# A two-layer hybrid decoder trunk: in the first feed-forward block the inverse root moves from GpSimd to Newton's steps on VectorE, the token sums stand earlier on TensorE, and VectorE gets another order of block sums and weight sums

## The chip, the cores and the metric

The kernel runs on one core of a Trainium2 chip. The metric is the device time of one execution in microseconds (us); of several runs the median is given. TensorE (PE) multiplies, VectorE (DVE), ScalarE (ACT) and GpSimd (POOL) work on tiles elementwise, and SyncE (SP) issues most transfers. Each engine takes its instructions in order, and an instruction starts when the semaphores that it waits for have been counted up.

## The reference

512 tokens of width 1024 pass two layers. Each layer is a gated feed-forward block, a mixer (a convolution module in layer 0, sparse attention in layer 1), a second feed-forward block and a gated embedding. What matters here is the very first block:

```python
def rms_norm(x, g):
    xf = x.astype(jnp.float32)
    y = xf * lax.rsqrt(jnp.mean(xf * xf, axis=-1, keepdims=True) + RMS_EPS)
    return (y * g.astype(jnp.float32)).astype(x.dtype)

def swiglu(x, wg, wu, wd):
    return (jax.nn.silu(x @ wg) * (x @ wu)) @ wd

x = x + 0.5 * swiglu(rms_norm(x, ffn1_norm[i]), ffn1_w_gate[i], ffn1_w_up[i], ffn1_w_down[i])
```

The inner width is 2816, that is 22 blocks of 128. All inputs are float32.

## The kernel before, in words

**Layout.** The tokens lie transposed: eight tiles `xs` of 128 features x 512 tokens. The norm's factor of a token is not put on the input. The input times the gain goes through the products, and the factor R (one number per token, spread over all partitions) multiplies the result.

**Precision.** Every float32 operand is split into a rounded part h and a rest l = x - h; a product is three matmuls, h·h, h·l and l·h (`mm3`, lines 356 to 358). ScalarE makes h by a copy with rounding and VectorE makes l by a subtraction. For weights these are lines 292 and 294 (tiles `raw` or `rawx` to `wh` and `wl`).

**The norm's factor.** `square_sum` squares the input tiles on ScalarE (line 430) and adds them up on VectorE (line 432) in the tile `acc`. `rfin` then goes in two stages. The first takes the sums over the features for each token, four matmuls of 128x1 (line 445, `token_sums`), adds 1e-6 (line 467, `v`) and raises to the power -0.5 on GpSimd (line 438, `r`). The second spreads r by four transposes on TensorE (line 451) and copies the result on ScalarE (line 458, `R`).

**Plain blocks and pairs.** The first two of the 22 inner blocks (`PLAIN`) are computed directly: gate and up, eight matmul triples each with 512 columns. When R is there, the gate is multiplied by it (line 600), ScalarE takes its Silu (line 601), VectorE multiplies by the up product (line 558), and the result is split (lines 560 and 561). The other blocks go in pairs by a scheme of seven products of 256 columns instead of eight (`pairs`). It needs block sums of the inputs, made once in a feed-forward block by `right_sums`: copies with the gain (line 480), differences (line 482), split in h and l (lines 490 and 491, tiles `px`). And it needs sums of the weights for each pair: `first_sums` and `combine`, lines 327, 328, 312 and 313 (tiles `sq` and `rawx`), split in lines 330 and 331 (`s1hl`) and 316 and 317. The products are called s (the weights themselves), c, e and d (sums of weights): two of s, two of c, one of e, two of d, for the gate and for the up block. Between them ScalarE copies a bank to the tile `G` (line 503) and VectorE adds (line 502).

**What sets the order.** The code is written in the order in which it wants things; a scheduler then merges this into one fixed queue for each engine by its own estimate of times, and `issue_after(x)` forbids it to place an instruction ahead of x. `high_priority` lifts a step. `ahead` splits weights some units (`HLB`, five buffers of h and l) before their product. The second tile of a pair (`rawx`, two buffers) is loaded again only when the last weight sum of the pair before was read. In the first feed-forward block nothing comes before: the program begins with it, and inputs, weights, squares, block sums and weight sums all arrive in the first 60 us.

## Time and profile before

| | us |
|---|---|
| median of 3 runs | 2021.34 (2021.1 to 2021.44) |
| the profiled execution | 2022.01 |
| its span, first to last instruction | 2020.2 |
| PE busy | 1994.7 (99%) |
| DVE busy | 1558.9 (77%) |
| ACT busy | 1100.5 (54%) |
| POOL busy | 330.7 (16%) |

A row of a timeline gives start and length in us, the engine, the line of the kernel, the operation, the tile written and the tiles read, the count of equal instructions put together, and, in brackets, how long the engine stood idle before and what released it. Consecutive instructions of one engine overlap a little, so the distance between two starts is the cost of the first. A matmul of 512 columns is listed with some 0.39 us though the next starts 0.23 us later. A row of stretches gives the limits, the length, busy time and count of instructions for PE, PEld (weight loads), DVE, ACT and POOL, then the TensorE clock that was granted as a share of full speed, the share of the DMA engines, and GB/s.

### The profile page before, as it was taken

Reading aid. Unit: us, or ns where it says so; the run is one execution under the profiler, and the core shown is the slowest. Engines: PE = TensorE matmul, PEld = TensorE weight load, DVE = VectorE, ACT = ScalarE, POOL = GpSimd, SP = SyncE. Lnnn points to the kernel's source line nnn. Section 1 sums busy time; section 2 is a strip of 40 time slices with the busy share of each in tenths; the row PEclk is TensorE's granted clock in tenths of the full one; section 3 lists DMA queues with packets and bytes.
Section 4 is the critical chain, followed back from the end, with each engine's and each line's share of the span. In section 5 each row is a group of like instructions: output and inputs, shape, how many; then the busy total and the mean of one; then the engine's idle time right before and its main releaser. Section 6 shows DMA issues by size and latency. Waiting matters only on the chain.

```text
span 2020.2 us, 32789 instructions
## 1 busy us (share of the span) xinstructions
PE 1994.7 (99%) x12534; PEld 1789.9 (89%) x12534; DVE 1558.9 (77%) x2751; ACT 1100.5 (54%) x1972; POOL 330.7 (16%) x365
## 2 busy tenths in 40 slices
PE   8999999999999999999999999999999999999998
PEld 7989899888789898988999989887888789898987
DVE  8869777795697796877968868647989796886875
ACT  7535445663565363545644525337888674463543
POOL 0000000352300000012000000557666200000022
PEclk9999999999999999999999999999999999999999
DMA  4332322466325243343232322463323023232241
GB/s 169 105 104 96 126 80 99 181 215 201 131 102 169 90 142 125 97 136 115 84 125 85 121 89 95 152 194 103 94 88 102 27 96 124 95 115 94 94 142 58
DMA packets 79485, 235.16 MB, mean 116 GB/s; under 512 B 8849, under 2 KB 16161, under 8 KB 79329
## 3 DMA queue, kind: packets, MB, share of 16 engines
q1 hardware_dynamic: 78368, 230.69, 34.6%
q8 instruction: 98, 1.61, 0.3%
q0 software_dynamic: 816, 2.33, 0.3%
q14 instruction: 59, 0.48, 0.1%
q10 hardware_dynamic: 144, 0.07, 0.0%
HBM read 214.66 MB, written 16.29 MB: 114 GB/s over the span
## 4 chain that ended last, share of the span: by engine, by line
PE 88%; DVE 8%; ACT 2%; issue 1%; DMA 1%; SPq 0%; DVEq 0%; POOL 0%; ACTq 0%
PE b L356 27%; PE b L357 27%; PE b L358 27%; PE b L821 2%; DVE t L1245 1%; PE b L1180 1%; PE b L1242 1%; PE b L1119 1%; DMA raw<-in_w 1%; DVE s L415 1%; DVE e L1198 1%; DVE t L482 1%; DVE wl L294 1%; DVE px L491 0%; DVE acc L432 0%
## 5 line engine op out<-in xcount | busy, mean ns | idle before, releaser
L356 PE MATMUL b<-s,wh 128*128 128x256 f32 (+1 forms) x1408 | 448.8, 320 | 1.6 <-ACT wh L292 1.0
L357 PE MATMUL b<-s,wh 128*128 128x256 f32 (+1 forms) x1408 | 447.8, 319 | 1.3 <-DVE s L415 0.9
L358 PE MATMUL b<-s,wl 128*128 128x256 f32 (+1 forms) x1408 | 445.9, 318 | 0.1
L292 ACT ACTIVATE wh<-raw 128x1024 fp32r<-128x1024 f32 (+1 forms) x251 | 263.8, 1054 | 256.4 <-PE b L357 171.6
L357 PE MATMUL b<-px,wh 128*128 128x256 f32 (+1 forms) x1112 | 321.0, 289 | 1.0 <-DVE px L491 0.8
L356 PE MATMUL b<-px,wh 128*128 128x256 f32 (+1 forms) x1112 | 321.1, 289 | 0.7 <-ACT G L503 0.7
L358 PE MATMUL b<-px,wl 128*128 128x256 f32 (+1 forms) x1112 | 321.0, 289 | 0.0
L294 DVE TENSOR_TENSOR wl<-raw,wh 128x1024 fp32r<-128x1024 f32 (+1 forms) x205 | 251.2, 1227 | 63.6 <-ACT wh L292 62.7
L356 PEld LDWEIGHTS b<-s,wh 128*128 128x128 f32 x1408 | 268.3, 191 | 21.0 <-ACT wh L292 1.6
L357 PEld LDWEIGHTS b<-s,wh 128*128 128x128 f32 x1408 | 268.1, 190 | 20.1 <-DVE s L415 2.5
L358 PEld LDWEIGHTS b<-s,wl 128*128 128x128 f32 x1408 | 267.4, 191 | 17.9 <-DVE wl L294 0.5
L358 PE MATMUL b<-hid,wl 128*128 128x512 f32 x704 | 275.2, 393 | 0.0
L357 PE MATMUL b<-hid,wh 128*128 128x512 f32 x704 | 275.0, 392 | 0.0
L356 PE MATMUL b<-hid,wh 128*128 128x512 f32 x704 | 269.3, 390 | 0.0
L294 POOL TENSOR_TENSOR wl<-raw,wh 128x1024 fp32r<-128x1024 f32 (+1 forms) x53 | 128.4, 2428 | 709.3 <-ACT wh L292 709.2
L503 ACT ACTIVATE G<-b 128x256 f32<-128x256 f32 x400 | 144.5, 376 | 142.6 <-PE b L358 126.9
L357 PEld LDWEIGHTS b<-px,wh 128*128 128x128 f32 x1112 | 209.1, 188 | 6.4 <-DVE px L491 1.4
L356 PEld LDWEIGHTS b<-px,wh 128*128 128x128 f32 x1112 | 209.2, 188 | 6.1 <-ACT G L503 1.3
L358 PEld LDWEIGHTS b<-px,wl 128*128 128x128 f32 x1112 | 208.8, 188 | 3.8
L357 PEld LDWEIGHTS b<-hid,wh 128*128 128x128 f32 x704 | 132.2, 188 | 29.2
L356 PEld LDWEIGHTS b<-hid,wh 128*128 128x128 f32 x704 | 132.2, 188 | 28.4
L358 PEld LDWEIGHTS b<-hid,wl 128*128 128x128 f32 x704 | 132.2, 188 | 27.3
(246 smaller groups left out, 3642.8 us busy)
## 6 DMA issues: line engine op xcount, KB each, us to landing
raw<-in_w SPq DMA_DIRECT2D x255, 512.0 KB, 3.3
rawx<-in_w SPq DMA_DIRECT2D x80, 512.0 KB, 3.2
tw<-in_tw SPq DMA_DIRECT2D x20, 576.0 KB, 6.7
skew<-table SPq DMA_DIRECT2D x16, 320.0 KB, 5.9
z<-t SPq DMA_DIRECT2D x16, 256.0 KB, 2.2
hid<-z SPq DMA_DIRECT2D x16, 256.0 KB, 4.0
tt<-skew SPq DMA_DIRECT2D x16, 256.0 KB, 3.1
wr<-in_w SPq DMA_DIRECT2D x8, 512.0 KB, 4.1
```

Source lines behind the costliest of these rows:

```text
L292: nc.scalar.activation(h[:, c], t[:, c], AF.Copy)
L294: eng.tensor_tensor(l[:, c], t[:, c], h[:, c].bitcast(F32), op=OP.subtract)
L356: mm(out, sh, mh, start=start, stop=False, **how)
L357: mm(out, sh, ml, start=False, stop=False, **how)
L358: self.lastmm = mm(out, sl, mh, start=False, stop=stop, **how).ins
L415: b = nc.vector.scalar_tensor_tensor(view(l), x, g, view(h.bitcast(F32)), op0=OP.mult, op1=OP.subtract)
L482: sub = lambda o, x, y: nc.vector.tensor_tensor(o, x, y, op=OP.subtract)
L503: copy = lambda o, x: nc.scalar.activation(o, x, AF.Copy)
L821: nc.tensor.matmul(p[:, q * SP:q * SP + SP], T[q][:, d * 128:d * 128 + 128], u[:, q, o:o + SP], start=d == 0, stop=d == LAGS - 1)
L1119: nc.tensor.matmul(P[mh][:, :124], w, B[kk // 4][:, kk % 4, :], start=kk == 0, stop=kk == 15)
L1180: nc.tensor.matmul(p[:, :32 - lo + nk], Q, KT[:, i, "sw".index(b), lo:32 + nk], start=i == 0, stop=i == 1)
L1198: nc.vector.tensor_tensor_reduce(out=dst, in0=src[b], in1=bias, scale=1.0, scalar=3e38, op0=OP.add, op1=OP.min, accum_out=mn[:, a, bi:bi + 1])
```

## The change

Only the first feed-forward block of layer 0 (`first`) is touched, in five places.

1. The root. `root_steps` replaces the power on GpSimd: an integer estimate and three Newton steps, ten VectorE instructions of 128x4 (lines 465 to 469 of the new kernel).
2. The token sums. The first stage of `rfin` is written ahead of the eighth input of the first two blocks, no longer behind the third input of the second gate block (`SUMS_AT` is gone). The second stage, the transposes, stays behind the second gate block.
3. The order of block sums and weight sums. For the first pair the weight sums are no longer made along with the split (`lazy`); they are made when the c weights are due, and their splits and the last sum stand behind the block sums (`issue_after(self.righted)`). `cap` limits how far weights are split ahead in the meantime. The four calls of `right_sums` wait for the accumulator's last addition (the first one) or the end of the root (the others).
4. The plain blocks' gates (R, Silu and so on) are written behind the block sums and the first products of the first pair instead of ahead of them.
5. Six buffers for temporaries (`tb`) in this block instead of four.

```diff
+NEWTON = 3
...
         if pair:
-            with self.behind():
-                self.first_sums(j)
+            if j not in self.lazy:
+                with self.behind():
+                    self.first_sums(j)
+                    self.sum_parts(j)
...
+        lazy = what == "c" and j in self.lazy
+        if lazy:
+            self.first_sums(j)
         q = self.sums[j]
         if what == "c":
             nc.vector.tensor_tensor(q[:, lo], u[:, lo], t[:, lo], op=OP.subtract)
-            nc.vector.tensor_tensor(u[:, lo], t[:, hi], q[:, lo], op=OP.subtract)
+            if not lazy:
+                nc.vector.tensor_tensor(u[:, lo], t[:, hi], q[:, lo], op=OP.subtract)
...
+        if lazy:
+            with self.tc.issue_after(self.righted):
+                self.sum_parts(j)
+                nc.vector.tensor_tensor(u[:, lo], t[:, hi], q[:, lo], op=OP.subtract)
...
+    def root_steps(self, v, n):
+
+        nc = self.nc
+        y = self.tiny.tile([128, 4], F32, name="r", tag="r")[:, :n]
+        a = self.tiny.tile([128, 4], F32, name="ra", tag="ra")[:, :n]
+        nc.vector.tensor_scalar(y.bitcast(I32), v.bitcast(I32), -0.5, float(0x5f3759df), op0=OP.mult, op1=OP.add)
+        for _ in range(NEWTON):
+            nc.vector.tensor_tensor(a, y, y, op=OP.mult)
+            nc.vector.scalar_tensor_tensor(a, a, -0.5, v, op0=OP.mult, op1=OP.mult)
+            self.root = nc.vector.scalar_tensor_tensor(y, a, 1.5, y, op0=OP.add, op1=OP.mult).ins
+        return y
...
-            r = self.rsqrt(v, 4)
+            r = (self.root_steps if steps else self.rsqrt)(v, 4)
...
+        first = (n, i) == (1, 0)
+        if first:
+            self.lazy = [PLACE[nm, i, 0, PLAIN][0] for nm in (g, u)]
+            self.cap = ENTRY["s", self.lazy[0]]
+        fin = self.rfin(self.acc, steps=first)
...
                             plain(pg, g, f, ks)
                             plain(pu, u, f, ks)
+                            if first and len(ks) > 1:
+                                with self.tc.issue_after(self.lastmm):
+                                    next(fin)
...
                 if first:
-                    with self.tc.issue_after(self.squared), self.tc.issue_after(self.vins):
-                        for k in range(KD // 2):
+                    for k in range(KD // 2):
+                        with self.tc.issue_after(self.squared), self.tc.issue_after(self.root if k else self.summed):
                             self.right_sums(f"ffn{n}_norm", i, k)
+                        if k == KD // 2 - 2:
+                            self.cap = ENTRY["s", self.lazy[1]] + 1
+                            with self.tc.issue_after(self.root):
+                                self.ahead(ENTRY["s", self.lazy[1]])
+                    self.cap = None
...
+                if first and f == PLAIN:
+                    with self.tc.issue_after(self.righted):
+                        plain_gates()
...
-            self.tb = 4
+            self.tb = 6 if i == 0 else 4
```

In the built programs the order differs on PE, DVE and ACT within the first feed-forward block alone; GpSimd loses the root, and SyncE's order is the same. Line numbers of the new kernel are larger: 375 to 377 are the old 356 to 358, 476 the old 445, 482 the old 451, 498 the old 467, 513 the old 482, 522 the old 491, 534 the old 503, 639 the old 601.

**PE, around the token sums.** Before, in the second gate block (`b_282`) and the second up block (`b_283`):

```order
L357 MATMUL b_282<-s_180,wh_138 128x512
L358 MATMUL b_282<-s_179,wl_139 128x512
L445 MATMUL b_301<-meanr,acc_183 128x1 x4
L451 MATMUL b_325<-ident,r 128x128 x4
L356 MATMUL b_283<-s_151,wh_144 128x512
```

Now, where the first two blocks (`b_206` and `b_207`) end with their eighth input (`s_179`, `s_180`) and the second gate block (now `b_281`) begins:

```order
L377 MATMUL b_206<-s_179,wl_125 128x512
L376 MATMUL b_207<-s_180,wh_132 128x512
L377 MATMUL b_207<-s_179,wl_133 128x512
L476 MATMUL b_256<-meanr,acc_183 128x1 x4
L375 MATMUL b_281<-s_151,wh_138 128x512
```

The token sums have moved up by the 24 matmuls of the second gate block; the transposes stay behind that block. In the built order the sums stand behind the eighth input of both first blocks.

**DVE, behind the accumulator's last addition.** Before (`acc_183`; then weight sums, splits, `v`, block sums):

```order
L432 TENSOR_TENSOR acc_183<-acc_183,t_203 128x512
L327 TENSOR_TENSOR sq_218<-raw_142,rawx_208 128x512
L328 TENSOR_TENSOR rawx_208<-rawx_208 128x512
L312 TENSOR_TENSOR sq_218<-rawx_208,raw_142 128x512
L294 TENSOR_TENSOR wl_145<-raw_136,wh_144 128x1024
L294 TENSOR_TENSOR wl_215<-raw_142,wh_214 128x1024
L331 TENSOR_TENSOR s1hl_221<-rawx_208,s1hl_221 128x512
L467 TENSOR_SCALAR v<-b_301 128x4
L482 TENSOR_TENSOR t_363<-G_362 128x512
```

Now, the accumulator's last addition is followed by the first block sums, `v` and the root's steps (`r` and `ra`); the third Newton step follows some rows further down:

```order
L451 TENSOR_TENSOR acc_183<-acc_183,t_203 128x512
L513 TENSOR_TENSOR t_339<-G_338 128x512
L513 TENSOR_TENSOR t_340<-G_338,t_339 128x256
L513 TENSOR_TENSOR t_340<-G_338,t_340 128x256
L498 TENSOR_SCALAR v<-b_256 128x4
L465 TENSOR_SCALAR r<-v 128x4
L467 TENSOR_TENSOR ra<-r 128x4
L468 SCALAR_TENSOR_TENSOR ra<-ra,v 128x4
L295 TENSOR_TENSOR wl_145<-raw_136,wh_144 128x1024
L469 SCALAR_TENSOR_TENSOR r<-ra,r 128x4
L467 TENSOR_TENSOR ra<-r 128x4
L522 TENSOR_TENSOR px_346<-t_339,px_346 128x512
```

The weight sums of the first pair have left this place for one behind the root; all eight block sums' splits (`px`) now stand ahead of the first gate times R.

**ACT, around the first Silu.** Before (the plain gate `b_206`, among weight splits `wh` and block sums `px`):

```order
L316 ACTIVATE wh_440<-rawx_208 128x1024
L601 ACT_TABLE_LOAD
L601 ACTIVATE t_418<-b_206 128x512
L316 ACTIVATE wh_473<-rawx_212 128x1024
L292 ACTIVATE wh_504<-raw_290 128x1024
L490 ACTIVATE px_401<-t_392 128x512
L490 ACTIVATE px_412<-t_405 128x512
L503 ACTIVATE G_439<-b_437 128x256
```

Now, between the copies (`G`) of the first pair's banks (`b_402`, `b_405`, and `b_403`, `b_406` for its other sums):

```order
L534 ACTIVATE G_407<-b_405 128x256
L639 ACT_TABLE_LOAD
L639 ACTIVATE t_634<-b_206 128x512
L534 ACTIVATE G_404<-b_402 128x256
L534 ACTIVATE G_407<-b_405 128x256
L639 ACTIVATE t_642<-b_281 128x512
L323 ACTIVATE wh_434<-rawx_208 128x1024
L323 ACTIVATE wh_467<-rawx_212 128x1024
L595 ACTIVATE hid_638<-b_207 128x512
L534 ACTIVATE G_404<-b_403 128x256
```

The table load and the Silu wait for the gate times R on VectorE, and the copies that the pair's next products need are now queued behind them.

## The prediction

> **What bounds the kernel now.** I read the page first, then the timeline of TensorE (PE) over the first 60 us, the stretches with their granted clock, and the timelines of VectorE (DVE) and ScalarE (ACT) beside it. The page gives the span, and 99% of it with PE busy.

> ```profile
> span 2020.2 us, 32789 instructions
> ```

> So what PE loses anywhere reaches the end, and a gain counts only as far as PE stays fed behind it. In PE's timeline (start, length, engine, line, tiles, count, idle time before) the change's place looks so:

> ```profile
> 20.81 0.39 PE L356 MATMUL b<-s,wh 128*128 128x512 f32 x1
> ...
> 26.25 0.95 PE L445 MATMUL b<-meanr,acc 128*128 128x1 f32 x8
> 29.87 1.12 PE L451 MATMUL b<-ident,r 128*128 128x128 f32 x4 [2.67 <-POOL r L438]
> 30.64 0.78 PE L356 MATMUL b<-s,wh 128*128 128x512 f32 x1
> ...
> 38.63 0.28 PE L356 MATMUL b<-s,wh 128*128 128x256 f32 x1
> ...
> 50.03 0.39 PE L356 MATMUL b<-px,wh 128*128 128x256 f32 x2
> 50.56 0.39 PE L357 MATMUL b<-px,wh 128*128 128x256 f32 x1
> 50.78 0.28 PE L358 MATMUL b<-px,wl 128*128 128x256 f32 x1
> 50.90 0.28 PE L357 MATMUL b<-px,wh 128*128 128x256 f32 x1
> 51.02 0.28 PE L358 MATMUL b<-px,wl 128*128 128x256 f32 x1
> 51.54 0.39 PE L356 MATMUL b<-px,wh 128*128 128x256 f32 x1 [0.24 <-ACT G L503]
> ```

> The second gate block (24 matmuls) runs from 20.81 to 26.25, so one of 512 columns costs 0.227 us. Then the token sums, and 2.67 us idle until GpSimd's root; the second up block follows at 30.64, and the products of the first pair of blocks (256 columns, 0.12 us each by 50.78 and 50.90) at 38.63. The idle time costs twice, as the stretches show (length, busy time of PE, PEld, DVE, ACT, POOL, then the granted clock):

> ```profile
> 25.60:29.01 3.41, 1.60 (x12) 1.40 (x10) 3.41 (x6) 0.06 (x1) 0.60 (x1) 1.00 0.40 139
> 29.01:35.84 6.83, 5.97 (x16) 4.88 (x17) 6.83 (x12) 5.84 (x9) 0.80 (x1) 0.50 0.26 85
> 1390.93:1394.35 3.42, 2.00 (x9) 1.28 (x7) 2.38 (x4) 3.42 (x10) 3.42 (x4) 1.00 0.04 14
> 1578.67:1582.08 3.41, 1.00 (x7) 0.55 (x5) 3.35 (x25) 3.36 (x15) 0.91 (x2) 1.00 0.16 65
> 1582.08:1588.90 6.82, 6.34 (x19) 4.56 (x20) 5.05 (x17) 5.90 (x25) 6.08 (x14) 0.50 0.01 4
> ```

> After a stretch with PE busy 1.60 of 3.41 us the clock is halved for 6.83 us, and late in the program once more after 1.00 of 3.41; after 2.00 of 3.42 it is not. PE works 5.97 us of the first halved stretch at half rate, so it loses 3.0 us there. Idle time and half rate together are some 5.6 us: the most that this change can reach for.

> But VectorE is busy in every moment of these two stretches (3.41 of 3.41, 6.83 of 6.83). PE's waits at 50.03 to 51.54 (0.3 us beyond its two matmuls, then 0.4, and 0.1 for each restart, 1.0 in all) already come from there and from ScalarE.

> **Part one: PE's path to the pairs.** The order shown above puts the token sums behind the first blocks' last matmul, not before their eighth input. They read the accumulator, whose last additions and what follows stand in VectorE's timeline:

> ```profile
> 19.81 2.28 DVE L432 TENSOR_TENSOR acc<-acc,t 128x512 f32<-128x512 f32 x3
> 23.23 0.69 DVE L327 TENSOR_TENSOR sq<-raw,rawx 128x512 f32<-128x512 f32 x1 [1.15 <-DMA raw<-in_w]
> ...
> 28.17 0.15 DVE L467 TENSOR_SCALAR v<-b 128x4 f32<-128x4 f32 x1
> 28.24 0.68 DVE L482 TENSOR_TENSOR t<-G 128x512 f32<-128x512 f32 x1
> ...
> 33.99 1.21 DVE L317 TENSOR_TENSOR wl<-sq,wh 128x1024 fp32r<-128x1024 f32 x1
> 35.13 0.68 DVE L482 TENSOR_TENSOR t<-G 128x512 f32<-128x512 f32 x1
> 35.73 1.28 DVE L600 TENSOR_TENSOR b<-b,R 128x512 f32<-128x512 f32 x2
> 36.93 0.41 DVE L482 TENSOR_TENSOR t<-G,t 128x256 f32<-128x256 f32 x1
> 37.26 1.28 DVE L491 TENSOR_TENSOR px<-t,px 128x512 fp32r<-128x512 f32 x2
> ```

> The accumulator is whole at 22.09. That is a new wait: PE, free at 20.81, stands 1.3 us, loads for some 0.15, and everything on its queue stands behind it. Then 0.95 for the sums (23.2), 5.44 for the gate (28.65), the transposes (0.77 at half rate; 0.4 at full), and 5.44 for the up block: the pairs start at 34.5 instead of 38.63, a gain of 4.1 us. The root must be there by 28.65. It is ten VectorE steps of 128x4 behind v. Such a step's cost is bounded by two rows: 0.07 where nothing waits (28.17 to 28.24) and 0.19 where the next needs it:

> ```profile
> 1344.97 0.15 DVE L1215 TENSOR_SCALAR sm<-sm 128x1 f32<-128x1 f32 x1
> 1345.16 0.16 DVE L1216 RECIPROCAL sm<-sm 128x1 f32<-128x1 f32 x1
> ```

> In the order four of the eleven (v counted) have a long instruction behind them, which hides their end, and seven have their reader: 4 times 0.07 and 7 times 0.19, 1.6 us (0.8 to 2.1 at the ends). With the long ones between (one split of 1.14, two px of 0.60) and the three block sums ahead (1.3), the root is there at 22.0 + 1.3 + 1.6 + 2.3 + 0.2 = 27.4. It hides behind the gate with 1.2 us to spare. GpSimd loses a step on which nothing else depends.

> **Part two: VectorE's queue to the first Silu.** What counts is when VectorE ends what PE needs next. Steps by the rows above: 0.60 for 512 columns, 0.33 for 256, 1.14 for 1024. From 22.0 to the first gate times R the new order has 4 block sums of 512 (2.4) and 8 of 256 (2.7), 8 px (4.8), 5 weight splits (5.7), 6 weight sums (3.6), 2 s1hl (1.2): 20.4. With 1.6 for the root, 0.2 for two waits on itself and 0.7 for the gate itself it ends at 44.9. VectorE starts at once on the block sums, where before it stood 1.15 us for a transfer; that pays for most of the root.

> **Part three: ScalarE behind it.** ScalarE's rows are

> ```profile
> 40.32 0.39 ACT L503 ACTIVATE G<-b 128x256 f32<-128x256 f32 x1 [1.80 <-PE b L358]
> 40.60 1.05 ACT L316 ACTIVATE wh<-sq 128x1024 fp32r<-128x1024 f32 x1
> 41.55 1.05 ACT L316 ACTIVATE wh<-rawx 128x1024 fp32r<-128x1024 f32 x1
> 42.62 1.28 ACT L601 ACT_TABLE_LOAD   x1
> 43.91 0.60 ACT L601 ACTIVATE t<-b 128x512 f32<-128x512 f32 x1
> ```

> In the new order the Silu of the plain gate stands ahead of the copies that free the first pair's banks. So: 44.9, table load 1.28, Silu 0.5 to the next start, copy 0.39: PE may go on with the third product (c, second half) at 47.2. PE is there earlier: 34.5, 48 matmuls for s (5.75), 24 for c (2.9, with 0.1 for its last px at 43.0), 24 for e (2.9): 46.1. First wait 1.1. That product runs to 50.1; the next needs a bank that ScalarE copies only after the second copy (0.3), second Silu (0.5), two splits (1.9), a hid (0.5) and the copy (0.4), from 47.0: 50.6. Second wait 0.6. Then VectorE again, from 46.9: up to the second pair's second c split it has 17 steps of 0.60, 6 of 0.33 and 7 of 1.14, 20.2 in all, without a pause: some 67.4. PE has 254 matmuls of 0.12 (30.4) ahead of it: 34.5 + 30.4 + 1.7 + 0.2 for restarts = 66.8. Third wait 0.6 to 0.7.

> **The sum.** 4.1 gained by the pairs' start; 1.0 of old waits gone; 1.1, 0.6 and 0.7 of new ones and 0.3 for restarts: 5.1 - 2.7 = 2.4 us. Behind that the instructions stand in the same order on every engine from the first down projections on, so PE carries it to the end. Six buffers instead of four for the temporaries cost no instruction; I take nothing for them. With the root at its ends the sum is 3.2 or 1.9. The profiled execution took 2022.01 (1.8 outside its span), 0.67 above the runs' median of 2021.34. It would come to 2019.6, and the median to **2018.9**. About 0.2% (4.0 us) is what a measurement can tell here from no change, so this counts as the same.

> **The rivals.** *The late halved stretch goes too.* PE's gap there ends at 1582.09 (stretch of 1.00 busy). If the stretches stand fixed against the start and the program comes 2.4 us earlier, the gap falls on both sides of 1578.67, and each side is busier than 1.00. Whether that is enough I can't read: 1.60 was too little, 2.00 not. For it: the three runs differ by only 0.34 us, as if all met the same stretches. Against: little work of PE fills the second side. It would save at most half of 6.34; say 3.0: 2.4 + 3.0 = 5.4, 2015.9. Chance 0.26.

> *The new gap halves the clock.* From 20.81 to 23.2 PE stands or does only token sums. With the stretches as in this run, 18.77 to 22.19 would hold 2.2 us of work and the next 2.4 without the sums, both above 2.00, so no. If they lay otherwise, one could hold as little as 1.1 besides the sums. Half rate for 6.83 us would cost PE 3.4, but the waits at 47, 51 and 67 (2.4) would swallow most: 34.5 + 3.4 + 30.4 + 0.1 = 68.4 against 67.5, so 1.5 gained, 2019.8. Chance 0.11. [...]

> *A reload that comes late (slower).* The second tiles of the next pair can be loaded only when the first pair's d splits have read the old ones: before, these loads were issued from 45.13 on,

> ```profile
> 45.13 2.40 SPq L244 DMA_DIRECT2D rawx<-in_w  x2
> ```

> and the page's list of loads gives 512 KB each and 3.2 us to landing, in the median:

> ```profile
> rawx<-in_w SPq DMA_DIRECT2D x80, 512.0 KB, 3.2
> ```

> Now they are issued, by the sum, at some 50.2 and 51.4, land at 53.4 and 54.6, and VectorE asks for them at 54.6 and 56.4. So they just come in time; each us beyond lengthens the third wait by one. From 2.4 us the gain is gone; from 6.4, a landing in three times the median, the change is slower by 0.2%. Chance 0.05 (0.04 for the full amount).

> **How the numbers follow.** The forecast has 0.58, own range 2018.1 to 2019.5. The range reaches down to the late stretch's case and up to the halved new gap: 2015.6 to 2020.4. Faster by over 0.2% is the late stretch and a small part of the rest where my new waits don't come: 0.29. Slower: 0.04. The same: 0.67.

> **What would show it.** Right: token sums at 22.2 to 22.4, no halved stretch before 60 us, transposes at once behind the gate, pairs from about 34.5, PE waits of about 1 us near 47 on ScalarE and half that near 51. Wrong: a wait of the transposes for the root, a clock of 0.50 between 22 and 36, or PE through to 70 us without a wait, by which VectorE's queue would be shorter than I counted. The late stretch is told by the clock near 1580.

## The result, and the profile after

The changed kernel takes **2034.37 us** (median of six, 2033.86 to 2036.86), the kernel before 2021.79 in six runs beside it: ratio 1.006, interval 1.0050 to 1.0071. It is slower by 12.6 us. The forecast was 2018.9, its range ended at 2020.4, and slower had a chance of 0.04. The prediction is wrong in its direction.

Yet the first feed-forward block, which all its steps were about, came out much as it said. The profiled execution took 2034.42, with

```profile
span 2032.6 us, 32782 instructions
```

Its timeline of TensorE (PE) around the change's place, against the rows of before that the prediction shows:

```profile
22.33 1.14 PE L476 MATMUL b<-meanr,acc 128*128 128x1 f32 x8 [1.18 <-DVE acc L451]
23.33 0.77 PE L375 MATMUL b<-s,wh 128*128 128x512 f32 x1
23.90 0.63 PE L376 MATMUL b<-s,wh 128*128 128x512 f32 x1
...
30.42 0.60 PE L482 MATMUL b<-ident,r 128*128 128x128 f32 x4
...
36.34 0.28 PE L375 MATMUL b<-s,wh 128*128 128x256 f32 x1
...
67.64 0.39 PE L377 MATMUL b<-px,wl 128*128 128x256 f32 x1 [0.47 <-DVE wl L324]
```

The token sums stand where they were forecast, after PE has waited 1.18 us for the accumulator (1.3 forecast); the transposes no longer wait for a root. But the gate's first two matmuls start 0.57 us apart and the next ones 0.43, where 0.23 is usual. The stretches (length, busy time of PE, PEld, DVE, ACT, POOL, granted clock, DMA share, GB/s) say why:

```profile
19.75:23.16 3.41, 2.23 (x15) 1.65 (x13) 3.17 (x6) 3.41 (x7) 0.00 (x0) 1.00 0.45 154
23.16:26.57 3.41, 3.41 (x10) 2.73 (x11) 3.24 (x12) 3.41 (x6) 0.00 (x0) 0.50 0.03 7
...
1589.88:1596.71 6.83, 6.15 (x18) 4.37 (x19) 5.03 (x17) 5.93 (x24) 6.04 (x15) 0.50 0.00 1
```

The new gap halves the clock as the old one did (0.50 behind the stretch with PE busy 2.23 of 3.41 us), though for 3.41 us and not for 6.83. That costs 1.7 us of work, and the pairs start at 36.34 where 34.5 was forecast. The late halved stretch stays. VectorE (DVE) takes the root's steps at the forecast price, some 0.2 us where the next one waits:

```profile
19.99 2.28 DVE L451 TENSOR_TENSOR acc<-acc,t 128x512 f32<-128x512 f32 x3
...
23.71 0.16 DVE L498 TENSOR_SCALAR v<-b 128x4 f32<-128x4 f32 x1
23.90 0.17 DVE L465 TENSOR_SCALAR r<-v 128x4 int32<-128x4 int32 x1
...
27.65 0.16 DVE L469 SCALAR_TENSOR_TENSOR r<-ra,r 128x4 f32<-128x4 f32 x1
```

The root is ready at 27.8 (27.4 forecast), and ScalarE (ACT) is released by the first gate times R at 45.29 (44.9 forecast):

```profile
45.29 1.28 ACT L639 ACT_TABLE_LOAD   x1 [3.89 <-DVE b L638]
```

So nothing in the first 70 us costs 12.6 us. Where the time goes is seen from the down projections. Each feed-forward block has an unbroken run of 192 matmuls with `hid` as the moving operand. Of before, four such runs, each from its first start to the start of the matmul behind it, with the busy time and the count of these matmuls alone:

```profile
223.09:267.04 43.95, 43.95 (x192) 1.00 0.26 85
769.46:813.41 43.95, 43.95 (x192) 1.00 0.32 101
1158.19:1202.14 43.95, 43.95 (x192) 1.00 0.25 84
1824.71:1868.65 43.94, 43.94 (x192) 1.00 0.26 85
```

Of after, the same four runs:

```profile
222.60:267.21 44.61, 44.61 (x192) 1.00 0.25 84
772.09:816.70 44.61, 44.61 (x192) 1.00 0.31 99
1164.81:1209.42 44.61, 44.61 (x192) 1.00 0.25 83
1833.96:1878.57 44.61, 44.61 (x192) 1.00 0.25 84
```

At the first run the new kernel is ahead by 0.49 us, then behind by 2.63, 6.62 and 9.25. And each run by itself is longer, 44.61 for 43.95, though no wait is in it, the clock is 1.00 in both and the instructions are the same: 44.61 us over 192 is 232.4 ns for each matmul, where it was 228.9. The block sums `px` (256 columns) lose more; of before and after, the last run of 120 of them:

```profile
1989.99:2003.59 13.60, 13.60 (x121) 1.00 0.01 1
```

```profile
2001.29:2015.52 14.23, 14.23 (x121) 1.00 0.00 1
```

That is 118.6 ns for 113.4. Over the program the mean distance of two starts, waits included, rises from 229.0 to 232.4 ns for 2112 matmuls with `hid` and from 117.5 to 120.1 for 3024 with `px` of 256 columns and `wh` or `wl`: 7.2 and 7.9 us, 15.1 in all. Less the 2.4 us that the first block was to gain this makes 12.7; measured are 12.6. That it fits so closely is luck, since two smaller terms are left out: 312 matmuls with `px` of 512 columns cost 1.0 us more, and 2880 with the inputs `s` of 256 columns 1.5 us less (120.1 and 119.6 ns).

### The profile page after: what moved, and what is told of

Same layout as the page of the kernel before. It is cut to its first block, busy times and chain, and to the rows that moved or that the text cites. A ratio compares the mean times of both kernels' runs of the same rounds, so it can differ in the third digit from the quotient of the medians.

```text
span 2032.6 us, 32782 instructions
## 1 busy us (share of the span) xinstructions
PE 2008.0 (99%) x12534; PEld 1796.5 (88%) x12534; DVE 1559.8 (77%) x2761; ACT 1100.7 (54%) x1972; POOL 330.0 (16%) x364
## 4 chain that ended last, share of the span: by engine, by line
PE 89%; DVE 6%; ACT 2%; DMA 1%; issue 1%; SPq 0%; DVEq 0%; POOL 0%; ACTq 0%
PE b L375 27%; PE b L377 27%; PE b L376 27%; PE b L866 2%; PE b L1225 1%; PE b L1287 1%; DMA raw<-in_w 1%; PE b L1306 1%; PE b L1164 1%; PE b L1307 1%; DVE t L1290 1%; DVE t L513 1%; DVE wl L324 1%; DVE px L522 0%; DVE wl L295 0%
## 5 line engine op out<-in xcount | busy, mean ns | idle before, releaser
L375 PE MATMUL b<-px,wh 128*128 128x256 f32 (+1 forms) x1112 | 324.8, 293 | 0.5 <-ACT G L534 0.5
L376 PE MATMUL b<-px,wh 128*128 128x256 f32 (+1 forms) x1112 | 324.2, 292 | 0.8 <-DVE px L522 0.8
L295 DVE TENSOR_TENSOR wl<-raw,wh 128x1024 fp32r<-128x1024 f32 (+1 forms) x205 | 251.2, 1226 | 66.8 <-ACT wh L293 66.2
L376 PE MATMUL b<-hid,wh 128*128 128x512 f32 x704 | 277.0, 395 | 0.0
L375 PE MATMUL b<-hid,wh 128*128 128x512 f32 x704 | 272.9, 395 | 0.0
## 6 DMA issues: line engine op xcount, KB each, us to landing
raw<-in_w SPq DMA_DIRECT2D x255, 512.0 KB, 3.3
rawx<-in_w SPq DMA_DIRECT2D x80, 512.0 KB, 3.3
wr<-in_w SPq DMA_DIRECT2D x8, 512.0 KB, 4.0
```

The lines of the kernel that those rows point to most:

```text
L295: eng.tensor_tensor(l[:, c], t[:, c], h[:, c].bitcast(F32), op=OP.subtract)
L375: mm(out, sh, mh, start=start, stop=False, **how)
L376: mm(out, sh, ml, start=False, stop=False, **how)
```

## The experiments

**Theory A: addresses.** The second small tile of the root, `ra`, takes two buffers of 32 bytes per partition in the pool `tiny`. That pool lies ahead of the tiles of each phase, so in the built program all of these (`px`, `hid`, `t`, `G` and so on) begin 64 bytes higher. `hid` goes from 0 to 64 modulo 512, `px` as well. The weights `wh` and `wl` and the inputs `s` lie ahead of `tiny` and stay at 192. **Theory B: the work.** The new order, six buffers or Newton's steps disturb something that lasts. The first four kernels tell these apart.

*b_pad64: the kernel before, with a tile that nothing reads.*

```diff
+        nc.gpsimd.memset(self.tiny.tile([128, 4], F32, name="pad", tag="pad", bufs=2), 0.0)
```

> The kernel before, its order of instructions kept, with an unused tile of the same size as the new kernel's second root tile (two buffers of 32 bytes per partition) in the same pool; one write of it on GpSimd at the start is the only instruction added. Every tile that a phase allocates lies 64 bytes higher, as in the new kernel. Theory A (the addresses cost the time): the drift of the new kernel without its gain in the first block, so 2021.8 + 12.6 + 2.4 = about 2036, matmuls with hid as moving operand start every 232 ns instead of 227 to 230, those with px every 120 instead of 117. Theory B (the new order, the six buffers or Newton's steps cost the time): 2021.8, nothing changed.

Measured: 2035.94 us, ratio 1.0070 (1.0056 to 1.0084). Two of its runs of matmuls, `hid` and `px`:

```profile
224.60:269.21 44.61, 44.61 (x192) 1.00 0.26 83
2002.67:2016.90 14.23, 14.23 (x121) 1.00 0.00 1
```

(Of the `px` run, here and below, one of the 121 only reaches into the stretch.) To the hundredth these are the lengths of the changed kernel. An unused tile does all of the damage, without one step of the change.

*b_pad32: the same with `bufs=1`.*

> The same with one buffer of the unused tile: every tile that a phase allocates lies 32 bytes higher. Theory A with a rule of 64 bytes (only tiles that begin on a multiple of 64 are fast, or only on a multiple of 128): slow, about 2036. Theory A with a cost that grows with the offset: between, some 2029. Theory B: 2021.8.

Measured: 2041.60 us, ratio 1.0096 (1.0082 to 1.0109), the slowest of all.

```profile
225.27:270.07 44.80, 44.80 (x192) 1.00 0.25 82
2008.97:2023.36 14.39, 14.39 (x121) 1.00 0.01 1
```

The idea that the cost grows with the offset falls: 32 bytes cost more than 64, 233.3 ns for `hid` and 119.9 for `px`.

*a_pad128: the changed kernel with the same padding line as b_pad64.*

> The new kernel with the same unused tile, two buffers: together with its own second root tile the phases' tiles lie 128 bytes higher than in the kernel before, so equal to it modulo 128. Theory A, if what counts is the address modulo 128: 2021.8 - 2.4 = 2019.4. Theory A, if it is the address itself or the distance to the tiles that are not moved: 2034 still. Theory B: 2034.4.

Measured: 2028.65 us, ratio 1.0032 (1.0019 to 1.0044). It is neither of the times expected.

```profile
221.51:266.31 44.80, 44.80 (x192) 1.00 0.25 83
1996.18:2009.79 13.61, 13.61 (x121) 1.00 0.00 1
```

At 128 `px` is as fast as at 0 (13.61 us for 13.60), but `hid` is as slow as at 32 (44.80 us in both). So an address modulo 128 isn't the rule, and the two operands have different good places. The sum fits: 2112 times 4.4 ns is 9.3 us over the next kernel's 2019.66.

*a_spare: the changed kernel without a second tile.* The root's tile takes 32 bytes in any case; its spare columns serve as scratch.

```diff
-        y = self.tiny.tile([128, 4], F32, name="r", tag="r")[:, :n]
+        y = self.tiny.tile([128, 8], F32, name="r", tag="r")[:, :n]
         self.root = self.nc.gpsimd.tensor_tensor(y, v, self.power[:, :n], op=OP.pow).ins
...
-        y = self.tiny.tile([128, 4], F32, name="r", tag="r")[:, :n]
-        a = self.tiny.tile([128, 4], F32, name="ra", tag="ra")[:, :n]
+        t = self.tiny.tile([128, 8], F32, name="r", tag="r")
+        y, a = t[:, :n], t[:, 4:4 + n]
```

> The new kernel with Newton's scratch in spare columns of the root's own tile (which takes 32 bytes in any case), so that no second tile is allocated and every tile that a phase allocates lies where it did before. Order, Newton's steps and six buffers stay. Theory A: 2021.8 - 2.4 = 2019.4, no drift behind the first block, matmuls with hid at 227 to 230 ns again. Theory B: 2034.4, unchanged.

Measured: 2019.66 us, ratio 0.9990 (0.9981 to 0.9999).

```profile
221.06:265.00 43.94, 43.94 (x192) 1.00 0.26 85
1987.92:2001.52 13.60, 13.60 (x121) 1.00 0.01 1
```

The drift is gone with the tile; order, Newton's steps and buffers are those of the changed kernel. Theory B falls. What is left of the change is 2.5 us (0.2 to 3.8 by the interval), which the prediction summed up as 2.4.

**Relative to what?** Two kernels ask whether the address itself counts or a distance, and to which tile.

*a_all64: a_spare with 64 bytes ahead of everything, weights included.*

```diff
+        nc.gpsimd.memset(self.cpool.tile([128, 16], F32, name="pad"), 0.0)
         self.small = self.cpool.tile([128, NSMALL], F32, name="small")
```

> The new kernel with Newton's scratch in the root's tile (as in the run before it) and 64 bytes of padding ahead of everything else: the phases' tiles, the inputs s and the weights wh and wl all lie 64 bytes higher, so their distances to one another are those of the kernel before. If the cost comes from the distance between the moving operand and the weights that are loaded beside it: 2019.7, hid at 229 ns and px at 117. If it comes from the address itself: hid and px as in the new kernel (232 and 120 ns), about 2034, and s may change too.

Measured: 2019.90 us, ratio 0.9990 (0.9981 to 0.9999), and the two runs as in a_spare:

```profile
220.59:264.54 43.95, 43.95 (x192) 1.00 0.26 86
1986.92:2000.52 13.60, 13.60 (x121) 1.00 0.00 1
```

With `hid` and `px` at 64 modulo 512, where they took 44.61 and 14.23 us in b_pad64, they take 43.95 and 13.60 here, with everything else moved along. So what counts in these runs is a distance.

*a_w448: a_spare with only the split weights moved.*

```diff
+        self.padded = False
...
+        if not self.padded:
+            self.wpool.tile([128, 112], F32, name="pad0", tag="pad0")
         h = self.wpool.tile([128, HU], F32R, name=f"wh{self.uid}", tag="wh", bufs=self.HLB)
         l = self.wpool.tile([128, HU], F32R, name=f"wl{self.uid}", tag="wl", bufs=self.HLB)
+        if not self.padded:
+            self.wpool.tile([128, 16], F32, name="pad1", tag="pad1")
+            self.padded = True
```

> The new kernel with Newton's scratch in the root's tile, order unchanged on every engine; only the split weights wh and wl are moved, by 448 bytes (from 192 to 128 modulo 512), and what lies behind them by 512. Nothing else changes its offset. The distance from the weights to hid and px is then modulo 512 that of the new kernel (384). If the weights are the partner: hid at 232 ns and px (with wh and wl) at 119 to 120, so 2112 times 3.5 and 3024 times 2.5, 15 us: about 2034; the distance of s (64) has not been run, so some us either way. If the partner is another tile (the temporaries, the unsplit weights) or none: 2019.7, hid at 229 and px at 117.

Measured: 2033.22 us, ratio 1.0057 (1.0041 to 1.0074).

```profile
222.29:267.09 44.80, 44.80 (x192) 1.00 0.25 83
2002.11:2016.35 14.24, 14.24 (x121) 1.00 0.00 1
```

The drift is back though no moving operand changed its offset modulo 512 to any tile but the weights. The partner is `wh` and `wl`. That it is PE's own reading of them is concluded from this: behind the start of this last `px` run, at 2002.11, VectorE, ScalarE and GpSimd have no instruction that names `wh`, `wl` or `raw`, and the DMA engines' share is 0.00, yet the run is as slow (14.24 us for 14.23 in the changed kernel). `px` has 118.7 ns for the 118.6 of distance 384 in the changed kernel; `hid` has 233.3 for 232.4, so the distance modulo 512 is not the whole rule. The sum was 15 us and 13.6 came, because `s` of 256 columns, now at distance 64, gains: 117.9 ns in the mean instead of 120.1, 6.3 us over 2880. `hid` and `px` lose 8.8 and 8.0, and the matmuls of `px` and `s` with 512 columns some 3.

**Can the placing be bettered?** `s` lies at the weights' own offset, distance 0, and its 512 columns start every 227 ns.

*a_hid192: a_spare with `hid` at distance 0.*

```diff
                 nc.vector.tensor_tensor(pu, pu, gr, op=OP.mult)
+                if f == 0:
+                    self.ptile("pad", 1, 48)
```

> The same kernel without that padding, but with 192 bytes ahead of the tiles hid alone, so that they begin at 192 modulo 512, as s, wh and wl do in every kernel; each engine's order is word for word that of the kernel without it. s with 512 columns starts every 226 to 227 ns at 192. If the offset sets the rate whatever the tile: hid falls from a mean of 229.0 to 226.5, 2112 times 2.5 ns is 5.3 us, so 2019.7 - 5.3 = 2014.4. If only multiples of 512 are good for hid: 233 ns as at 32 and 128, 2112 times 4.2 is 8.9 us, so 2028.6.

Measured: 2016.11 us, ratio 0.9971 (0.9961 to 0.9980): 3.6 us less than a_spare, where 5.3 were expected.

```profile
220.54:264.08 43.54, 43.54 (x192) 1.00 0.27 88
```

226.8 ns, the rate of `s`. Over all 2112 the mean is 226.9, so 4.4 us would be due; the rest is within the scatter.

*a_s0: besides, `s` at `px`'s distance, 320.*

```diff
+        self.padded = False
...
+        if not self.padded:
+            self.spool.tile([128, 80], F32, name="spad", tag="spad")
+            self.tiny.tile([128, 24], F32, name="tpad", tag="tpad")
+            self.padded = True
         t = self.spool.tile([128, 512], dt, name=f"s{self.uid}", tag="s", bufs=NSLOT)
```

> The kernel with hid at 192 modulo 512, and besides it the inputs s moved by 320 bytes, from 192 to 0 modulo 512, where px lies; all that lies behind s moves by 512 in all, so the distances of px and hid to the weights stay modulo 512. Order unchanged on every engine. If the distance sets the rate for every tile: s with 256 columns goes from 120 to px's 117.4, 2880 times 2.6 ns is 7.5 us saved; s with 512 columns goes from 226.7 to the 229 that hid had there, 1344 times 2.3 is 3.1 us lost; 2016.1 - 4.4 = 2011.7. If the rate belongs to the tile or to what runs beside it: 2016.1, s at 120 and 227.

Measured: 1998.44 us, ratio 0.9883 (0.9867 to 0.9900). The sign was right, the size not: 17.7 us less than a_hid192 instead of 4.4. A run of 48 matmuls with `s` of 256 columns before,

```profile
1868.66:1874.41 5.75, 5.75 (x48) 1.00 0.26 91
```

and one such run in this kernel:

```profile
1847.25:1852.91 5.66, 5.66 (x48) 1.00 0.30 93
```

Here a matmul fell by only 2 ns, as expected; most other runs fell further, and the mean over all 2880 goes from 120.1 to 114.8 (15.3 us). `px`, whose distance modulo 512 is unchanged, goes from 117.5 to 115.8 as well (5.1 us), and `s` with 512 columns gets slower by 1.4 ns (1.8 us). That is 18.6 us; 17.7 came.

The reason lies in two rates at this distance. The same 12 matmuls with `px`, of a_hid192 first and then of a_s0:

```profile
280.89:282.31 1.42, 1.42 (x12) 1.00 0.52 92
```

```profile
278.30:279.66 1.36, 1.36 (x12) 1.00 0.82 226
```

That is 118 and 113 ns, in the same order and at the same distance modulo 512. Counted in threes over the program, those of `px` with `wh` and `wl` go at the faster rate in 39% of the cases in a_hid192 and in 78% here; `s` has it here in 70%. What chooses between the two rates stays open.

*b_s0: the kernel before with the two paddings of a_s0.*

> The kernel before, order unchanged on every engine, with the placing of the run before this one (s at 0, hid at 192 modulo 512). If placing and change add up: the placing gave 2019.7 - 1998.4 = 21.3 us, so 2022.0 - 21.3 = 2000.7, and the change keeps its 2.3 us in this layout. If the change's gain came from its layout too: the same time as that run, 1998.4.

Measured: 1997.97 us, ratio 0.9883 (0.9868 to 0.9898). The placing is worth 23.5 us to the old kernel, and the change nothing measurable beside it, which is the time of the second case. The profile of b_s0 shows one reason: here the old gap halves no clock. Its wait and the stretches:

```profile
29.34 0.65 PE L456 MATMUL b<-ident,r 128*128 128x128 f32 x4 [2.40 <-POOL r L443]
...
35.32 0.28 PE L361 MATMUL b<-s,wh 128*128 128x256 f32 x1
```

```profile
24.51:27.92 3.41, 2.43 (x16) 2.06 (x14) 3.41 (x6) 0.61 (x2) 0.05 (x1) 1.00 0.25 65
27.92:31.34 3.42, 2.00 (x11) 1.75 (x12) 3.42 (x7) 2.64 (x4) 1.36 (x1) 1.00 0.58 198
31.34:34.75 3.41, 3.41 (x17) 2.79 (x16) 3.41 (x6) 3.28 (x7) 0.00 (x0) 1.00 0.12 47
```

The gap falls on both sides of 27.92, each side is busy for 2.00 us or more, and the pairs start at 35.32, 3.3 us earlier than in the profile of before and 1.0 earlier than in a_s0's (36.29). At the first long run of `hid` the two are level, at 218.26 and 218.19. Whether that holds in its other runs isn't known.

**The prediction's own steps.** Two kernels test what it said of the first 70 us.

*a_early: a_spare with PE's gap closed.*

```diff
-                            if first and len(ks) > 1:
-                                with self.tc.issue_after(self.lastmm):
-                                    next(fin)
...
-                        plain(p, nm, f)
-                        if p is pg:
+                        n1 = (2 if p is pg else 3) if first else KD
+                        plain(p, nm, f, range(n1))
+                        if first or p is pg:
                             with self.tc.issue_after(self.lastmm) if first else nullcontext():
                                 next(fin)
+                        with self.tc.issue_after(self.tsum) if first else nullcontext():
+                            plain(p, nm, f, range(n1, KD))
```

(`tsum` is the last of the token sums.)

> The new kernel with Newton's scratch in the root's tile, and with the token sums behind the second input of the second gate block and the transposes near the end of the second up block. VectorE's order is the same, and v comes at the same time, since the sums still wait for the accumulator only. But PE has no gap before the sums: the wait of 1.2 us and the halved clock of 3.4 us (some 1.8 us of work) go, and the pairs start 3 us earlier. If VectorE's queue sets PE's pace up to 70 us, as in the prediction: PE waits longer at 47 to 67 us and the time is that of the kernel without this edit, 2019.7. If PE's own path counts: 2016.7.

Measured: 2020.02 us, ratio 0.9990 (0.9981 to 0.9998). PE's timeline:

```profile
22.76 1.02 PE L476 MATMUL b<-meanr,acc 128*128 128x1 f32 x8
...
33.74 0.28 PE L375 MATMUL b<-s,wh 128*128 128x256 f32 x1
...
41.97 0.39 PE L377 MATMUL b<-px,wl 128*128 128x256 f32 x1 [0.61 <-DVE wl L324]
...
50.50 0.38 PE L375 MATMUL b<-s,wh 128*128 128x256 f32 x1 [0.51 <-ACT G L534]
63.08 0.38 PE L377 MATMUL b<-px,s1hl 128*128 128x256 f32 x1 [0.67 <-DVE s1hl L348]
66.62 0.39 PE L377 MATMUL b<-px,wl 128*128 128x256 f32 x1 [0.43 <-DVE wl L324]
```

No gap, no halved clock (1.00 in the stretches from 17.51 to 27.75), pairs 2.6 us earlier than in a_spare (36.38), and nothing gained: PE's waits between 41 and 69 us, two shorter ones of 0.23 and 0.29 among them, come to 2.7 us, where a_spare has 0.8. VectorE starts the gate times R 0.3 us later than in a_spare (44.56):

```profile
44.85 1.29 DVE L638 TENSOR_TENSOR b<-b,R 128x512 f32<-128x512 f32 x2
```

*a_tb4: a_spare with four buffers for temporaries.*

```diff
-            self.tb = 6 if i == 0 else 4
+            self.tb = 4
```

> The new kernel with Newton's scratch in the root's tile and four buffers for temporaries in the first feed-forward block instead of six. If six buffers do nothing, as the prediction took it: 2019.7. If two more buffers let VectorE run ahead of waits: slower by what it then waits, at most a few us, up to 2022. Tiles move by multiples of 4096 bytes, so theory A expects no drift.

Measured: 2020.73 us, ratio 0.9992 (0.9983 to 1.0001); a_spare's interval overlaps it. The six buffers cost nothing and give nothing that shows. This is not the buffers alone: the scheduler's order moves with them, on PE in 256 of 12534 places.

## Why the prediction was wrong, point by point

**The step that failed** is "Behind that the instructions stand in the same order on every engine from the first down projections on, so PE carries it to the end". The order is the same, but the same instructions do not take the same time. The prediction took every matmul's price from rows of before and never asked what a new tile does to the places of the others. b_pad64 shows that this alone makes the kernel slower by 13.8 us in its own comparison, and a_spare that without it the change is faster by 2.5. It put the price of what it did not touch at no change without a reason. None of the rivals held it; the only slower one was a late reload, and VectorE shows no wait for a transfer between 44 and 72 us. "Six buffers ... I take nothing for them" was right (a_tb4). The allocation to look at was the tile of four columns.

**The net of the sum was right**, 2.4 forecast and 2.5 measured by a_spare, though the interval (0.2 to 3.8) can't tell 2.4 from its neighbours, **with two terms off that cancel.** The pairs gain 2.3 us instead of 4.1, as the new gap halves the clock; this rival had 0.11. That was too low: of the seven profiles with this very order of PE four have the early halved stretch (after, a_spare, a_hid192, a_s0), three have none (a_all64, a_w448, a_pad128). The argument against it counted 2.2 us of work in a stretch and set it beside 2.00, which did not halve. The trace has 2.23 and did: without the token sums, matmuls of one column that fill the stretch from 22.33 on, 1.4 are left. That they don't count as work is argued, not shown. PE's busy time as the profile gives it, by which the prediction judged, doesn't decide it: late in a_pad128 stretches with 1.72 (1581.74 to 1585.16) and 1.97 (1585.16 to 1588.57) keep the clock, and the one behind them, with 2.35, is followed by 0.50.

The stretches do not lie at the same times in every run. In before and in after the clock's changes are whole steps of 3.413 us apart: 453 steps from 35.84 to 1582.08, and 458 from 26.57 to 1589.88. Here are a_all64's stretches, counted in such steps from that trace's own changes of the clock, with the same order and a gap of the same length (1.17 us, in after 1.18):

```profile
19.02:22.43 3.41, 2.24 (x13) 1.59 (x11) 3.20 (x5) 3.41 (x7) 0.00 (x0) 1.00 0.44 150
22.43:25.84 3.41, 3.41 (x19) 2.90 (x19) 3.20 (x11) 3.41 (x6) 0.00 (x0) 1.00 0.04 11
```

They end at 22.43 instead of 23.16, before most of the token sums, and the clock stays at 1.00. In after it was halved behind a stretch of 3.41 us with 1.18 of waiting and most of the token sums in it.

**The waits** were forecast at 1.1, 0.6 and 0.7 us, near 47, 51 and 67 us. With PE 1.8 us late there was none at 47 and 51, and 0.47 at 67: as that rival said, they swallow what the clock takes. a_all64, whose clock is not halved, shows the case that was forecast:

```profile
34.42 0.28 PE L375 MATMUL b<-s,wh 128*128 128x256 f32 x1
...
47.19 0.38 PE L375 MATMUL b<-px,wh 128*128 128x256 f32 x1 [0.81 <-ACT G L535]
50.61 0.39 PE L375 MATMUL b<-s,wh 128*128 128x256 f32 x1 [0.33 <-ACT G L535]
67.33 0.39 PE L377 MATMUL b<-px,wl 128*128 128x256 f32 x1 [0.50 <-DVE wl L324]
```

The pairs start at 34.42 (34.5 forecast), and all three waits are there, on the engines that were named, each 0.1 to 0.3 us short. In part that is addition: 46.9 + 20.2 is 67.1, not 67.4, which leaves 0.3 to 0.4 for the third, and the first comes to 1.0. Of the 2.0 us by which its pairs are ahead of a_spare's, 0.5 is left at the first long run of `hid` (220.59 and 221.06), and the two kernels take the same time (2019.90 and 2019.66). a_early shows the other half, that an earlier PE gains nothing as long as VectorE's queue sets the pace up to 70 us.

**The root, VectorE's queue, the table load** came within 0.4 us. **The late halved stretch** (0.26) stayed, 6.83 us long.

## What to carry to other kernels

A new tile is part of a change, however small: list where the old tiles begin before and after, and when a change costs a steady per cent in code that it doesn't touch, compare the same unbroken run of matmuls in both traces. Give scratch the spare bytes of a tile that is there, or pad so that nothing else moves. And a good placing of moving operands against weights was worth 21 us (a_s0 against a_spare) to 23.5 us (b_s0 against before) here, some ten times what the change was after.

## What the runs showed of the hardware

| distance | 512 columns | 256 columns | in |
|---|---|---|---|
| 0 | 226.8 ns (`hid`) | 119.8 ns (`s`) | a_hid192, before |
| 64 | 228.9 ns (`s`) | 117.7 ns (`s`) | a_w448 |
| 320 | 228.9 ns (`hid`) | 113.4 ns (`px`) | before |
| 352 | 233.3 ns (`hid`) | 119.9 ns (`px`) | b_pad32 |
| 384 | 232.4 and 233.3 ns (`hid`) | 118.6 and 118.7 ns (`px`) | after, a_w448 |
| 448 | 233.3 ns (`hid`) | 113.4 ns (`px`) | a_pad128 |

At 320 and 448 other runs with 256 columns are slower than the one in the table: the mean over all of `px` with `wh` and `wl` is 117.5 ns in before as in a_pad128, since part of them go at some 118. Of the places in the table the best differs with the number of columns: 0 for 512 (226.8 ns); for 256, 320 and 448 do equally well (113.4 ns). It is the columns and not the tile that count: 37 matmuls with `px` of 512 columns near the end take 8.47 us at distance 320 (before) and 8.64 at 448 (a_pad128), slower there as `hid` is. That the price is set between the stream of columns and the weights that PE loads beside it is argued from a_w448, where in the last `px` run PE alone touches the weights, and from the equal lengths of equal runs; it is not shown, since no run takes the weight loads away. Not tried: distances between 0 and 320 other than 64, and larger moduli; that 512 is the right one is the author's assumption.
